# Delta-rule heads with q, k and v projected in a row, k turned later, and adaLN quarters closed in two jobs

## The chip, the cores and the metric

The kernel runs on one core of one Trainium2 chip. A core has TensorE (matmuls and transposes, PE in the profile; its weight loads are PEld), VectorE (DVE), ScalarE (ACT), GpSimd (POOL) and SyncE (SP, which issues most DMAs). Each works through its own queue of instructions in order, and they wait for each other on semaphores. The metric is the device time of one execution in microseconds; of several runs the median counts.

## The reference, cut to what matters

The program is a trunk of two layers over 512 latent tokens behind 256 context tokens, 768 columns in all, with a model width of 2048. Each layer modulates and normalises its input (adaLN), multiplies it by one wide projection matrix, feeds the result to three groups of heads (retention, gated DeltaNet, latent attention), gates each group, and multiplies by an output projection. The change touches the four DeltaNet heads of each layer and the adaLN products. A DeltaNet head is, in the reference:

```python
qkv = jax.nn.silu(centred_dwconv(jnp.concatenate([q, k, v], axis=-1), conv_w))
...
q = l2norm(q) * GDN_HD ** -0.5
k = l2norm(k)
...
kb = k * beta[..., None]
a = jnp.where(strict, jnp.einsum('bhncd,bhnsd->bhncs', kb, k) * decay, 0.0)
rhs = jnp.concatenate([v * beta[..., None], kb * jnp.exp(gc)[..., None]], axis=-1)
sol = lax.linalg.triangular_solve(a + jnp.eye(CHUNK, dtype=f32), rhs, left_side=True,
                                  lower=True, unit_diagonal=True)
```

The convolution has five taps along the tokens. After these lines a scan over the chunks follows, in both directions, with q, k and `sol`. adaLN is a product of the conditioning vectors `c` and `c_ctx` with a 2048 x 6144 matrix in each layer, which gives scale, shift and gate.

## The kernel before, in words

**Numbers and tiles.** Data is float32. For TensorE each operand is split in a high and a low half, and a product is three matmuls: high by high, high by low, low by high. Weights come by DMA as `raw` tiles of 128x512; ACT writes the high half (`wh`, L227) and DVE the low one (`wl`, L228). The normalised input stands in on-chip memory as such halves (`hh`, `hl`). A projection of 128 output rows (`proj_in`, L284 and L286) goes through 16 steps, one for each block of 128 input rows. Each step has six matmuls if the context is needed: three of 512 columns for the latent tokens into `zl`, three of 256 for the context into `zc`. That is 96 matmuls for one projection, or *one tile* in what follows.

**A DeltaNet head** is `gdn_head`. `conv_in` projects, copies the result out of PSUM (`cz`, the context half by DVE, the latent half by ACT at L372), convolves it (the middle tap on ACT at L744, the four others as eight DVE instructions at L751) and applies silu (`ce`, with an exponential on ACT at L396, and a last product on DVE at L400). `gdn_head` calls it for q, then k, then v:

- After q, ACT squares `qT` into `lsq` (L763), and six small matmuls by a column of ones give the sums `ss` (L767).
- After k, six transposes bring `kr` into `knp` with tokens as rows (`turn`, L661). ACT sums the squares, a reciprocal root follows on ACT and DVE (`nss`, `nry`, `nrt`, L375 to L380), and DVE scales to `kn` (L664). Six transposes turn it back into `ktp`, and ACT copies that to `kT` (L778).
- After v, six transposes give `vnp`, copied to `vn`. DVE then writes the exponents `et` and `es` of the decays (12 instructions of each at L803 and L805), and ACT takes their exponentials.
- Then `kkp` (kT by kT on TensorE), `A` (DVE, L820), `Xt` (L833), and the inverse in levels, whose first matmuls are `vtp` (L845). A scan over six chunks in both directions and a normalisation end the head.

**The order of the work.** The kernel is written as Python calls; a scheduler gives each instruction a place in its engine's queue. Work called earlier has precedence, and an instruction whose inputs come later lets later work by. Weight loads run at raised precedence. The mixer phase calls `kr_ab`, four DeltaNet heads and four retention heads, and behind each some of a list `fill` of projections that need no head (query and key compressions, gates, retention's operands): 7, 6, 4 and 5 behind the DeltaNet heads. `gate` of the DeltaNet branch's first output block is called inside head 0 after v. TensorE so finds tiles of other projections to work on while a head's small steps run on DVE and ACT. Head 0 of layer 0 finds its q, k and v projections done in an earlier phase. In layer 1 the heads need q for the latent tokens only.

**adaLN beside the projections.** The 2048 x 6144 products for later use run as 64 jobs, one by each call of `ada_job`, which stands in the middle of every projection (between steps 8 and 9). A job loads parts of the matrix (`araw`), multiplies them on ACT (`ada_p`, L474) and adds them on POOL (`ada_a`, L476). Every fourth job completes a quarter of scale, shift or gate, and the next call of `ada_job` closes it in `ada_close`: matmuls by ones into `ada_z` (L497), a copy to `ada_e` on ACT (L501), four matmuls `ada_q` that turn it (L504), and a DVE add (L505). The jobs end inside layer 0, in its output projection.

Of the kernel before, what the change touches and what calls it, by code (L numbers as in the profile page):

```python
# [20 lines left out]
P = 128  # L21
# [11 lines left out]
C_GDN = 2048  # L33
# [68 lines left out]
def trunk(  # L102
# [19 lines left out]
    def pz(name="z"):  # L122
        return ps.tile([P, 512], F32, name=name, tag="z", bufs=3)

    def pm(name="m"):
        return ps.tile([P, 1024], F32, name=name, tag="m", bufs=2)
# [365 lines left out]
    def ada_close(l, n0):  # L492
        z = pz("ada_z")[:, :256]
        for i, acc in enumerate(ada_accs):
            for v in range(2):
                g = 2 * i + v
                T.matmul(z[32 * g:32 * g + 32], lhsT=ones[:, :32], rhs=acc[:, v], start=True, stop=True,  # L497
                         tile_position=(0, 32 * g))
        ada_accs.clear()
        e = wp.tile([P, 256], F32, name="ada_e", tag="ada_e", bufs=2)  # L500
        S.copy(e, z)  # L501
        q = pz("ada_q")
        for j in range(2):
            T.matmul(q[:, 4 * j:4 * j + 4], lhsT=e[:, j * P:(j + 1) * P], rhs=sel4, start=True, stop=True)  # L504
        V.tensor_tensor(out=ada_t[l][:, n0:n0 + 4, :].rearrange("p (i j) v -> p i j v", j=2),  # L505
                        in0=q[:, :8].rearrange("p (j i v) -> p i j v", j=2, i=2),
                        in1=par[l, 0][:, n0:n0 + 4].rearrange("p (i j) -> p i j", j=2).unsqueeze(3).to_broadcast([P, 2, 2, 2]), op=ALU.add)
        ada_scale(l, n0, 4)

    def ada_job():  # L510
        if 1 in ada_state:
            ada_close(*ada_state.pop(1))
        job = next(ada_jobs, None)
        if job:
            ada_run(job)
# [91 lines left out]
    def phase_a(l, hs):  # L607
        last = l == DEPTH - 1
        parB = par[l, 1]
        if True:  # L610
# [7 lines left out]
            def gate(c0, j):  # L618
                lo_ctx = not last
                zl, zc = proj_in(l, (c0), hs, lo_ctx)  # L620
                z, e = ev("gz"), ev("ge")
                lo = 0 if lo_ctx else NX
                evac(z, zl, zc)
                silu_mul(z[:, lo:], z[:, lo:], e[:, lo:])
                dma(out=gate_d[l][j][:, lo:], in_=z[:, lo:])
# [37 lines left out]
            def scale_tokens(dst, src, r, c0):  # L663
                V.tensor_tensor(out=c6(dst)[:, c0:], in0=c6(src)[:, c0:],  # L664
                                in1=r[:, c0:].unsqueeze(2).to_broadcast([P, NCH - c0, P]), op=ALU.mult)
# [71 lines left out]
            def conv_in(dst, c0, grp, need_ctx):  # L737
                zl, zc = proj_in(l, c0, hs, need_ctx)
                z = ev("cz")
                lo = 0 if need_ctx else NX  # L740
                evac(z, zl, zc)
                y = mk("cy")
                w = lambda j: parB[:, 12 * j + grp:12 * j + grp + 1]
                S.activation(out=y[:, lo:NT], in_=z[:, lo:NT], func=AF.Copy, scale=w(2))  # L744
                for j in (0, 1, 3, 4):
                    o = j - 2
                    for a, b in ((0, NX), (NX, NT)):
                        if a < lo:
                            continue
                        a_, b_ = max(a, a - o), min(b, b - o)  # L750
                        V.scalar_tensor_tensor(out=y[:, a_:b_], in0=z[:, a_ + o:b_ + o], scalar=w(j),  # L751
                                               in1=y[:, a_:b_], op0=ALU.mult, op1=ALU.add)
                e = mk("ce")
                silu_mul(dst[:, lo:NT], y[:, lo:NT], e[:, lo:NT])

            def gdn_head(h, gs):
                be, gcol, egl, ekd, nbe = gs
                qT = pt("qT")
                qlo = NX if last else 0
# [1 line left out]
                qv = tiny("qv")  # L761
                sq = mk("lsq")
                S.activation(out=sq[:, qlo:NT], in_=qT[:, qlo:], func=AF.Square)  # L763
                m = pm("ss")
                c0 = qlo // P
                for n in range(c0, NCH):
                    T.matmul(m[:, n:n + 1], lhsT=sq[:, n * P:(n + 1) * P], rhs=ones[:, 0:1], start=True, stop=True)  # L767
                V.tensor_scalar(out=qv[:, c0:], in0=m[:, c0:NCH], scalar1=EPS, scalar2=EPS * HD, op0=ALU.add, op1=ALU.mult)
                kr = mk("kr")
                conv_in(kr, C_GDN + 512 + h * P, 4 + h, True)  # L770
                kT, kn = pt("kT"), pt("kn")
                m = pm("knp")
                turn(m, kr, 0)
                r = token_rstd(m, 0, kr, lambda ss: V.tensor_scalar(out=ss, in0=ss, scalar1=EPS, scalar2=None, op0=ALU.add))
                scale_tokens(kn, m, r, 0)
                m = pm("ktp")
                turn(m, kn, 0)
                S.copy(kT, m[:, :NT])  # L778
                vT = mk("vT")
                conv_in(vT, C_GDN + 1024 + h * P, 8 + h, True)  # L780
                if h == 0:
                    gate(C_GDN + 1536, 4)

                vn = pt("vn")
                m = pm("vnp")
                for n in range(NCH):
# [269 lines left out]
            fill = cq + gg[1:2] + ckv + gg[2:3] + rr[0] + gg[3:] + rr[1] + rr[2] + rr[3] + mg  # L1056
            nf = [7, 6, 4, 5, 3, 3, 4, 4]
            for i, n in enumerate(nf):
                (gdn_head if i < 4 else ret_head)(*((i, gs) if i < 4 else (i - 4,)))
                for f in fill[sum(nf[:i]):sum(nf[:i + 1])]:  # L1060
                    f()

    def phase_b(l):
# [313 lines left out]
```

## Time and profile before

| | |
|---|---|
| median of 3 runs | 3215.6 us (3211.18 to 3217.71) |
| the profiled execution | 3222.98 us, of it 3221.2 us span |
| granted TensorE clock, mean over the span | 0.976 |
| TensorE busy | 3053.8 us, 95% |
| TensorE's weight loads | 2589.3 us, 80% |
| DVE busy | 2031.1 us, 63% |
| ACT busy | 1657.0 us, 51% |
| POOL busy | 697.1 us, 22% |

Busy shares are of the span. The granted clock is a share of full speed; TensorE runs at one of two levels, 2.4 GHz or 1.2 GHz, and a value between them is a mean over a stretch. In an answer, `PE x <- ACT y` means that TensorE's instruction writing x sat idle until ACT had written y. The times of a timeline count from the start of the span. The 3222.98 us of the profiled execution lie 7.4 us over the median.

### The profile page before, as it was taken

Reading aid. Unit: us, or ns where it says so; the run is one execution under the profiler, and the core shown is the slowest. Engines: PE = TensorE matmul, PEld = TensorE weight load, DVE = VectorE, ACT = ScalarE, POOL = GpSimd, SP = SyncE. Lnnn points to the kernel's source line nnn. Section 1 sums busy time; section 2 is a strip of 40 time slices with the busy share of each in tenths; the row PEclk is TensorE's granted clock in tenths of the full one; section 3 lists DMA queues with packets and bytes.
Section 4 is the critical chain, followed back from the end, with each engine's and each line's share of the span. In section 5 each row is a group of like instructions: output and inputs, shape, how many; then the busy total and the mean of one; then the engine's idle time right before and its main releaser. Section 6 shows DMA issues by size and latency. Waiting matters only on the chain.

```text
span 3221.2 us, 50805 instructions
## 1 busy us (share of the span) xinstructions
PE 3053.8 (95%) x18925; PEld 2589.3 (80%) x18925; DVE 2031.1 (63%) x3524; ACT 1657.0 (51%) x3492; POOL 697.1 (22%) x487
## 2 busy tenths in 40 slices
PE   6998989989889999999999999999999999999998
PEld 3576878878778878899888888888898888888887
DVE  3269568477577566766763355867585767766644
ACT  3266555654555656544677645442424245544534
POOL 0036344443443544000268700000000000000000
PEclk8999999989999999999999999999999999999999
DMA  8763433423424545512465542322323256512444
GB/s 286 257 193 115 122 103 99 133 66 92 134 79 141 159 144 159 159 48 60 136 216 164 160 122 66 98 72 61 102 58 99 74 149 186 147 54 62 134 118 129
DMA packets 496655, 399.22 MB, mean 124 GB/s; under 512 B 45367, under 2 KB 433047, under 8 KB 496407
## 3 DMA queue, kind: packets, MB, share of 16 engines
q1 hardware_dynamic: 496083, 395.87, 41.5%
q8 instruction: 148, 2.42, 0.3%
q14 instruction: 101, 0.82, 0.1%
q0 software_dynamic: 96, 0.02, 0.0%
q10 hardware_dynamic: 227, 0.08, 0.0%
HBM read 340.90 MB, written 54.97 MB: 123 GB/s over the span
## 4 chain that ended last, share of the span: by engine, by line
PE 53%; POOL 2%; ACT 2%; DMA 2%; DVE 2%; issue 1%; SPq 0%; ACTq 0%; POOLq 0%; DVEq 0%
PE zl L284 21%; PE zlc L284 7%; PE zc L286 5%; PE vz L267 4%; PE sc L1157 3%; POOL ada_a L476 2%; PE oacc L1216 2%; PE zt L275 2%; PE zlc L286 1%; PE ptp L1209 1%; PE racc L1037 1%; DMA araw<-in_ada_w_dram 1%; PE f L284 1%; ACT ada_p L474 1%; DMA gb<-g_d 0%
## 5 line engine op out<-in xcount | busy, mean ns | idle before, releaser
L476 POOL TENSOR_TENSOR ada_a<-ada_a,ada_p 128x512 f32<-128x512 f32 x480 | 695.1, 1448 | 1144.8 <-ACT ada_p L474 1098.7
L228 DVE TENSOR_TENSOR wl<-raw,wh 128x512 fp32r<-128x512 f32 x632 | 486.3, 771 | 421.2 <-ACT wh L227 333.1
L227 ACT CAST wh<-raw 128x512 fp32r<-128x512 f32 x632 | 377.8, 605 | 562.0 <-PE zc L286 208.3
L284 PE MATMUL zl<-hh,wh 128*128 128x512 f32 (+1 forms) x1440 | 581.4, 404 | 1.9 <-ACT hh L227 1.8
L284 PE MATMUL zl<-hl,wh 128*128 128x512 f32 (+1 forms) x1440 | 581.3, 404 | 1.0 <-DVE hl L228 1.0
L284 PE MATMUL zl<-hh,wl 128*128 128x512 f32 (+1 forms) x1440 | 581.3, 404 | 0.0
L474 ACT ACTIVATE ada_p<-araw,const_f 128x256 f32<-128x256 f32 x960 | 423.4, 501 | 64.7 <-DMA araw<-in_ada_w_dram 41.3
L284 PEld LDWEIGHTS zl<-hh,wh 128*128 128x128 f32 (+1 forms) x1440 | 274.0, 190 | 64.9 <-issue 3.8
L284 PEld LDWEIGHTS zl<-hh,wl 128*128 128x128 f32 (+1 forms) x1440 | 274.1, 190 | 58.6 <-issue 1.1
L284 PEld LDWEIGHTS zl<-hl,wh 128*128 128x128 f32 (+1 forms) x1440 | 273.8, 190 | 58.6 <-DVE hl L228 2.5
L286 PE MATMUL zc<-hh,wh 128*128 128x256 f32 (+1 forms) x960 | 279.6, 291 | 6.1 <-ACT ce L372 4.9
L286 PE MATMUL zc<-hl,wh 128*128 128x256 f32 (+1 forms) x960 | 277.9, 289 | 0.0
L286 PE MATMUL zc<-hh,wl 128*128 128x256 f32 (+1 forms) x960 | 277.8, 289 | 0.0
L286 PEld LDWEIGHTS zc<-hh,wh 128*128 128x128 f32 (+1 forms) x960 | 183.8, 191 | 14.6 <-ACT ce L372 6.7
L286 PEld LDWEIGHTS zc<-hh,wl 128*128 128x128 f32 (+1 forms) x960 | 184.3, 192 | 3.4 <-issue 2.9
L286 PEld LDWEIGHTS zc<-hl,wh 128*128 128x128 f32 (+1 forms) x960 | 184.5, 192 | 2.6 <-issue 0.8
L284 PE MATMUL zlc<-mh,wl 128*128 128x512 f32 x448 | 178.6, 399 | 0.0
L284 PE MATMUL zlc<-mh,wh 128*128 128x512 f32 x448 | 178.0, 397 | 0.0
L284 PE MATMUL zlc<-ml,wh 128*128 128x512 f32 x448 | 177.3, 396 | 0.0
L751 DVE SCALAR_TENSOR_TENSOR cy<-cz,const_f,cy 128x511 f32<-128x511 f32 (+3 forms) x176 | 141.8, 859 | 17.8 <-ACT cy L744 17.3
L284 PEld LDWEIGHTS zlc<-mh,wh 128*128 128x128 f32 x448 | 84.9, 189 | 20.4 <-ACT ada_p L474 0.8
L284 PEld LDWEIGHTS zlc<-ml,wh 128*128 128x128 f32 x448 | 84.8, 189 | 19.0
(1250 smaller groups left out, 6419.3 us busy)
## 6 DMA issues: line engine op xcount, KB each, us to landing
raw<-in_w_in_dram SPq DMA_DIRECT2D x368, 256.0 KB, 3.6
araw<-in_ada_w_dram SPq DMA_DIRECT2D x256, 256.0 KB, 3.4
raw<-in_w_out_dram SPq DMA_DIRECT2D x144, 256.0 KB, 3.8
ar<-in_ada_w_dram SPq DMA_DIRECT2D x128, 256.0 KB, 5.1
x_d<-xt SPq DMA_DIRECT2D x32, 384.0 KB, 3.6
raw<-in_w_in_dram SPq DMA_DIRECT2D x72, 128.0 KB, 3.4
ret_d<-rw SPq DMA_DIRECT2D x20, 384.0 KB, 2.8
rz<-ret_d SPq DMA_DIRECT2D x20, 384.0 KB, 3.5
```

Of the source, the lines that this page charges most:

```text
L227: S.copy(hi, src)
L228: V.tensor_tensor(out=lo, in0=src, in1=hi.bitcast(F32), op=ALU.subtract)
L267: T.matmul(z[:, 256 * i:256 * i + 256], lhsT=x_[:, (j + i) * P:(j + i + 1) * P], rhs=w, start=first and k == 0 and i == 0, stop=end and k ...
L275: T.matmul(z, lhsT=w, rhs=xx[:, a:b], start=own and first and k == 0, stop=own and last and k == nk - 1)
L284: T.matmul(zl[:m], lhsT=w, rhs=xx[:, NX:], start=st, stop=sp)
L286: i = T.matmul(zc[:m, :NX], lhsT=w, rhs=xx[:, :NX], start=st and zc_open, stop=sp and zc_open)
L474: S.activation(out=pr[:, v], in_=raw[:, i, :], func=AF.Copy, scale=cs32[:, 2 * k + v:2 * k + v + 1])
L476: G.tensor_tensor(out=acc, in0=acc, in1=pr, op=ALU.add)
L751: V.scalar_tensor_tensor(out=y[:, a_:b_], in0=z[:, a_ + o:b_ + o], scalar=w(j), in1=y[:, a_:b_], op0=ALU.mult, op1=ALU.add)
L1037: T.matmul(acc[:, :NL], lhsT=a[:, sl], rhs=b[:, :NL], start=st and i == 0, stop=sp and i == NCH - 1)
L1157: T.matmul(m[:, po:po + n], lhsT=a[:, qs], rhs=b[:, ko:ko + n], start=i == 0, stop=i == len(ops) - 1)
L1216: T.matmul(acc[:, os], lhsT=a[:, sl], rhs=b[:, js], start=j == 0 and n == 0, stop=j == nk - 1 and n == 2)
```

## The change

The program computes the same. Three things move:

- In `gdn_head` the column sums `ss` are called after k's projection and convolution instead of before, and v's after that; only then comes the turning of k into `knp` and `kn`. What is left of k (`ktp`, `kT`) and v's turn follow after one tile of other projections.
- That tile is the new argument `between`: for head 0 the `gate` that stood in it already, for the others the first entry of the head's own share of `fill`.
- `ada_close` ends after the copy to `ada_e`. The `ada_q` matmuls and the add are a function of their own, `ada_turn`, which the following call of `ada_job` runs.

```diff
@@ -499,6 +499,9 @@
         ada_accs.clear()
         e = wp.tile([P, 256], F32, name="ada_e", tag="ada_e", bufs=2)
         S.copy(e, z)
+        return l, n0, e
+
+    def ada_turn(l, n0, e):
         q = pz("ada_q")
         for j in range(2):
             T.matmul(q[:, 4 * j:4 * j + 4], lhsT=e[:, j * P:(j + 1) * P], rhs=sel4, start=True, stop=True)
@@ -508,8 +511,10 @@
         ada_scale(l, n0, 4)
 
     def ada_job():
+        if 2 in ada_state:
+            ada_turn(*ada_state.pop(2))
         if 1 in ada_state:
-            ada_close(*ada_state.pop(1))
+            ada_state[2] = ada_close(*ada_state.pop(1))
         job = next(ada_jobs, None)
         if job:
             ada_run(job)
@@ -753,7 +758,7 @@
                 e = mk("ce")
                 silu_mul(dst[:, lo:NT], y[:, lo:NT], e[:, lo:NT])
 
-            def gdn_head(h, gs):
+            def gdn_head(h, gs, between):
                 be, gcol, egl, ekd, nbe = gs
                 qT = pt("qT")
                 qlo = NX if last else 0
@@ -761,26 +766,24 @@
                 qv = tiny("qv")
                 sq = mk("lsq")
                 S.activation(out=sq[:, qlo:NT], in_=qT[:, qlo:], func=AF.Square)
+                kr = mk("kr")
+                conv_in(kr, C_GDN + 512 + h * P, 4 + h, True)
                 m = pm("ss")
                 c0 = qlo // P
                 for n in range(c0, NCH):
                     T.matmul(m[:, n:n + 1], lhsT=sq[:, n * P:(n + 1) * P], rhs=ones[:, 0:1], start=True, stop=True)
                 V.tensor_scalar(out=qv[:, c0:], in0=m[:, c0:NCH], scalar1=EPS, scalar2=EPS * HD, op0=ALU.add, op1=ALU.mult)
-                kr = mk("kr")
-                conv_in(kr, C_GDN + 512 + h * P, 4 + h, True)
+                vT = mk("vT")
+                conv_in(vT, C_GDN + 1024 + h * P, 8 + h, True)
                 kT, kn = pt("kT"), pt("kn")
                 m = pm("knp")
                 turn(m, kr, 0)
                 r = token_rstd(m, 0, kr, lambda ss: V.tensor_scalar(out=ss, in0=ss, scalar1=EPS, scalar2=None, op0=ALU.add))
                 scale_tokens(kn, m, r, 0)
+                between()
                 m = pm("ktp")
                 turn(m, kn, 0)
                 S.copy(kT, m[:, :NT])
-                vT = mk("vT")
-                conv_in(vT, C_GDN + 1024 + h * P, 8 + h, True)
-                if h == 0:
-                    gate(C_GDN + 1536, 4)
-
                 vn = pt("vn")
                 m = pm("vnp")
                 for n in range(NCH):
@@ -1056,8 +1059,12 @@
             fill = cq + gg[1:2] + ckv + gg[2:3] + rr[0] + gg[3:] + rr[1] + rr[2] + rr[3] + mg
             nf = [7, 6, 4, 5, 3, 3, 4, 4]
             for i, n in enumerate(nf):
-                (gdn_head if i < 4 else ret_head)(*((i, gs) if i < 4 else (i - 4,)))
-                for f in fill[sum(nf[:i]):sum(nf[:i + 1])]:
+                mine = fill[sum(nf[:i]):sum(nf[:i + 1])]
+                if i < 4:
+                    gdn_head(i, gs, gg[0] if i == 0 else mine.pop(0))
+                else:
+                    ret_head(i - 4)
+                for f in mine:
                     f()
 
     def phase_b(l):
```

Line numbers shift: L767 becomes L774, L774 L781, L778 L786, L664 L669, L751 L756, L803 L806. The order of the projections on TensorE is the same tile by tile; the small steps stand elsewhere between their matmuls. Counted in matmuls of a 96-matmul tile, `ss` moves in heads 1 to 3 of layer 0 from the 81st of k's tile to its end, `knp` from the 74th of v's tile to its end, `ktp` from the 5th of the fill tile to its end, `vnp` from the 81st to 85th of the fill tile to its end, `kkp` from there to the 3rd of the tile behind. `vtp` moves in that next tile from the 61st to the 48th in head 1 and from the 77th to the 58th in head 2. `ada_q` stood 5 matmuls behind `ada_z`; now at least half a tile lies between them. SP's and POOL's queues keep their order but for a few rows.

Three places show it, all in head 2 of layer 0. The first is TensorE's queue around `ss`, at the end of k's projection. Before:

```order
L286 MATMUL zc<-hh_1342,wh 128x256
L284 MATMUL zl<-hl_1343,wh 128x512
L767 MATMUL ss<-const_f,lsq 128x1 x6
L286 MATMUL zc<-hl_1343,wh 128x256
L284 MATMUL zl<-hh_1342,wl 128x512
L286 MATMUL zc<-hh_1342,wl 128x256
```

Now; the last two rows belong to v's projection:

```order
L284 MATMUL zl<-hl_1359,wh 128x512
L286 MATMUL zc<-hl_1359,wh 128x256
L284 MATMUL zl<-hh_1358,wl 128x512
L286 MATMUL zc<-hh_1358,wl 128x256
L774 MATMUL ss<-const_f,lsq 128x1 x6
L284 MATMUL zl<-hh_617,wh 128x512
L284 MATMUL zl<-hl_618,wh 128x512
```

`ss` stood inside the 14th of the 16 steps of k's tile and now stands behind the 16th.

The second is DVE's queue around `kn`. `kr` is k after silu, `vT` v after silu, `cy` the convolution's sum, `cz` a projection out of PSUM. Before:

```order
L400 TENSOR_TENSOR kr<-cy,ce 128x768
L228 TENSOR_TENSOR wl<-raw,wh 128x512
L774 TENSOR_SCALAR nss<-nss 128x6
L378 TENSOR_TENSOR nrt<-nrt,nss 128x6
L379 TENSOR_SCALAR nrt<-nrt 128x6
L380 TENSOR_TENSOR nss<-nry,nrt 128x6
L664 TENSOR_TENSOR kn<-knp,nss 128x768
L228 TENSOR_TENSOR wl<-raw,wh 128x512
L371 TENSOR_SCALAR cz<-zc 128x256
L751 SCALAR_TENSOR_TENSOR cy<-cz,const_f,cy 128x254
```

Now:

```order
L756 SCALAR_TENSOR_TENSOR cy<-cz,const_f,cy 128x510
L781 TENSOR_SCALAR nss<-nss 128x6
L228 TENSOR_TENSOR wl<-raw,wh 128x512
L395 SCALAR_TENSOR_TENSOR ce<-cy,ce 128x768
L378 TENSOR_TENSOR nrt<-nrt,nss 128x6
L379 TENSOR_SCALAR nrt<-nrt 128x6
L380 TENSOR_TENSOR nss<-nry,nrt 128x6
L669 TENSOR_TENSOR kn<-knp,nss 128x768
L400 TENSOR_TENSOR vT<-cy,ce 128x768
L806 SCALAR_TENSOR_TENSOR et<-gb,const_f 128x128
```

k's normalisation stood ahead of v's taps and now stands between v's last tap and `vT`.

The third is ACT's queue around `kT`'s copy. `rw<-zl` is the evacuation of the fill tile. Before:

```order
L227 CAST wh<-raw 128x512
L372 ACTIVATE cz<-zl 128x512
L474 ACTIVATE ada_p<-araw,const_f 128x256 x3
L778 COPY kT<-ktp 128x768
L744 ACTIVATE cy<-cz,const_f 128x768
```

Now:

```order
L396 ACTIVATE ce<-ce 128x768
L227 CAST wh<-raw 128x512
L474 ACTIVATE ada_a<-araw,const_f 128x256 x2
L474 ACTIVATE ada_p<-araw,const_f 128x256 x2
L811 ACTIVATE et<-et 128x768
L227 CAST wh<-raw 128x512
L372 ACTIVATE rw<-zl 128x512
L786 COPY kT<-ktp 128x768
L791 COPY vn<-vnp 128x768
L810 ACTIVATE es<-es 128x768
```

The copy stood ahead of v's first tap and now stands behind the fill tile's evacuation, directly ahead of v's own copy.

## Rows read from the trace of the kernel before

**Rows 1.** The page, first part: busy us, share of the span, instructions.

```profile
PE 3053.8 (95%) x18925; PEld 2589.3 (80%) x18925; DVE 2031.1 (63%) x3524; ACT 1657.0 (51%) x3492; POOL 697.1 (22%) x487
```

**Rows 2.** Stretches: us, busy of PE, PEld, DVE, ACT, POOL; clock, DMA, GB/s.

```profile
200.00:1250.00 1050.00, 952.93 (x6238) 823.82 (x6237) 716.85 (x1082) 612.90 (x1377) 467.94 (x322) 0.95 0.41 119
1600.00:1880.00 280.00, 268.35 (x1534) 230.28 (x1535) 123.14 (x155) 177.34 (x386) 190.10 (x133) 0.98 0.54 170
1950.00:2770.00 820.00, 811.72 (x5200) 689.06 (x5200) 561.64 (x1093) 351.11 (x706) 0.00 (x0) 1.00 0.37 102
```

**Rows 3.** Waits of TensorE from 200 to 1250 us: total, times, longest.

```profile
PE ss L767 <- ACT lsq L763: 21.5, 4, 5.7
PE knp L661 <- DVE kr L400: 17.5, 3, 6.0
...
PE ada_q L504 <- ACT ada_e L501: 7.0, 3, 2.9
```

**Rows 4.** Waits of TensorE from 1600 to 1880 us, layer 0's output projection.

```profile
PE ada_q L504 <- ACT ada_e L501: 8.0, 4, 3.9
```

**Rows 5.** Stretches, q's last to v's last matmul, heads 1 to 3.

```profile
412.80:464.80 52.00, 40.64 (x211) 35.30 (x210) 33.45 (x37) 30.24 (x70) 23.00 (x16) 0.87 0.28 80
636.80:689.60 52.80, 41.66 (x211) 36.08 (x210) 33.80 (x38) 30.30 (x71) 23.24 (x16) 0.84 0.23 66
842.00:894.70 52.70, 41.19 (x211) 35.76 (x210) 34.73 (x37) 30.28 (x72) 24.71 (x18) 0.84 0.30 86
```

**Rows 6.** Stretches, v's last matmul to `vtp`; the fourth in layer 1.

```profile
464.80:503.30 38.50, 34.19 (x195) 29.47 (x194) 34.12 (x62) 25.70 (x48) 20.41 (x14) 0.96 0.25 69
689.60:727.00 37.40, 33.45 (x223) 29.76 (x221) 30.93 (x60) 25.30 (x48) 21.70 (x12) 0.95 0.24 64
894.70:935.80 41.10, 34.98 (x206) 29.59 (x204) 33.96 (x63) 26.07 (x49) 16.96 (x13) 0.96 0.23 64
...
2322.20:2349.60 27.40, 27.26 (x184) 24.67 (x182) 23.52 (x60) 15.13 (x22) 0.00 (x0) 1.00 0.04 11
```

**Rows 7.** TensorE's timeline: start, duration, instruction, [idle before <- releaser].

```profile
395.94 0.40 PE L284 MATMUL zl<-hh,wh 128*128 128x512 f32 x1
...
397.00 0.40 PE L284 MATMUL zl<-hh,wh 128*128 128x512 f32 x1
...
656.70 2.50 PE L767 MATMUL ss<-const_f,lsq 128*128 128x1 f32 x11 [5.46 <-ACT lsq L763]
...
682.89 1.51 PE L661 MATMUL knp<-const_f,kr 128*128 128x128 f32 x6 [5.68 <-DVE kr L400]
```

**Rows 8.** ACT's timeline, head 2 of layer 0.

```profile
637.33 0.59 ACT L372 ACTIVATE cz<-zl 128x512 f32<-128x512 f32 x1
...
655.80 0.84 ACT L763 ACTIVATE lsq<-qT 128x768 f32<-128x768 f32 x1
...
691.79 0.78 ACT L778 COPY kT<-ktp 128x768 f32<-128x768 f32 x1
```

**Rows 9.** DVE's timeline, head 2 of layer 0.

```profile
687.37 0.58 DVE L378 TENSOR_TENSOR nrt<-nrt,nss 128x6 f32<-128x6 f32 x1 [1.06 <-ACT nrt L377]
...
689.36 0.96 DVE L664 TENSOR_TENSOR kn<-knp,nss 128x768 f32<-128x768 f32 x1
...
706.69 0.96 DVE L400 TENSOR_TENSOR vT<-cy,ce 128x768 f32<-128x768 f32 x1 [0.98 <-ACT ce L396]
...
718.45 0.34 DVE L820 SCALAR_TENSOR_TENSOR A<-kkp,const_f,es 128x128 f32<-128x128 f32 x1
```

**Rows 10.** What ended idle time before `ada_q`, 690 to 720 us: us, times.

```profile
  ACT ada_e L501: 2.3, 1
```

**Rows 11.** DVE groups (busy, mean ns, idle): 640-950, then 2280-2500 us.

```profile
L751 DVE SCALAR_TENSOR_TENSOR cy<-cz,const_f,cy 128x511 f32<-128x511 f32 x12 | 19.2, 1603 | 0.0
...
L751 DVE SCALAR_TENSOR_TENSOR cy<-cz,const_f,cy 128x511 f32<-128x511 f32 x12 | 9.0, 748 | 0.1
```

## The prediction

> **What bounds the kernel.** I read the busy times first. TensorE is busy for 95% of the span, DVE, the next engine, for 63% (weight loads aside) [rows 1], and the change adds and removes no matmul. What can be won is time in which TensorE waits or runs at its lower clock. So the second view is the stretches: 1050 us of layer 0's mixer phase hold 97 us without a matmul and a granted clock of 0.95; the stretch with the output projection of layer 0 holds 12 us at 0.98; 820 us of layer 1's mixer phase hold 8 us at 1.00 [rows 2]. Third, the waits of layer 0: first come `ss`, the column sums of q's squares (21.5 us, 4 times), then `knp`, k's first transposes (17.5 us, 3 times), then, after smaller ones, `ada_q` (7.0 us, 3 times) [rows 3]. The change is aimed at all three. In the output projection `ada_q` is by far the largest wait: 8.0 us in 4 waits [rows 4].
>
> Head 0 of layer 0 finds its projections done ahead and is a case by itself; heads 1 to 3 are alike. From the last matmul of q to the last matmul of v they need 52.0, 52.8 and 52.7 us with 40.6 to 41.7 us of matmul and a clock of 0.84 to 0.87 [rows 5]. From there to the first inverse matmul (`vtp`) they need 38.5, 37.4 and 41.1 us, at 0.95 to 0.96 [rows 6]. In layer 1, without the adaLN work, head 2 needs 27.4 us for the latter, and TensorE is idle for 0.1 us of it [rows 6].
>
> **q, k, v in a row.** A projection with context has 16 steps of 1.06 us (397.00 − 395.94) [rows 7], 17.0 us. In head 2, q's last matmul is at 636.8; its evacuation on ACT starts at 637.33 and `lsq` ends at 655.80 + 0.84 = 656.64 [rows 8]: a chain of 19.8 us. Before, `ss` stood behind 81 of k's 96 matmuls, and TensorE waited 5.46 us [rows 7]; now it stands behind all 96, so some 17.0 us lie in front of it and 2.8 us of wait remain. `ss` itself took 2.5 us at the half clock [rows 7], 1.3 at the full one. Then v runs, 17.0 us, with `knp` now behind all 96 of its matmuls instead of 74. k's chain is about as long as q's, and it begins late on DVE, whose queue still holds qT and two products with it when k ends; but `ss` has given it 4 us more. I take no wait at `knp`. A wait of 2.8 us still costs some clock: stretches with 4 to 6 us of idle time show 0.95 to 0.96, so 1.5 to 1.9 us are lost [rows 6]; I take 1.7. New stretch: 17.0 + 2.8 + 1.3 + 17.0 + 1.7 = 39.8 us, against 52.5 on average. **Gain 3 × 12.7 = 38 us.** If k's late start shows at `knp` (3.5 us a head), 27; if neither wait is left, 51.
>
> **Turning k and v.** Now v's chain carries k's tail. On DVE the steps from `nrt` to `kn` take 690.32 − 687.37 = 2.95 us [rows 9], and they stand between v's `ce` and vT, partly beside an exponential of v on ACT for which DVE waited 0.98 us before [rows 9]: vT comes 1.9 us later. After vT nothing is saved by the order: 24 `et`/`es` rows, the fill tile's evacuation, then `A`. Before, `A` came 718.45 − 707.65 = 10.8 us after vT, two weight splits included [rows 9]; now one split and one 0.4 us evacuation lie there, 8 to 9 us. On ACT kT's copy (0.78 us [rows 8]) stands behind the exponential of `et`, which must wait for about half of these 24 rows; I put it 6.4 us after vT. `kkp` then waits some 5 us on TensorE, but DVE reaches `A` only 2 us later, so most of this wait is time that would have been lost at `vtp`. The stretch to `vtp` so stays as long as it was, about 39 us: later vT and earlier `A` cancel. What is lost is work: `vtp` now stands 58 instead of 77 matmuls into the next tile in head 2, 48 instead of 61 in head 1, and head 3 is like them, about 2.2 us at the pace of [rows 7]. **Loss 3 × 2.2 = 6.6 us** (nothing if `A` comes 2 us earlier; 20 if v's chain grows by 4.5 us a head).
>
> The fill tile is no extra work: the projections follow each other on TensorE as before, only the small steps stand elsewhere. Its DMAs and adaLN jobs keep their places to a few rows on SP, and the POOL adds keep their order. Head 0 of layer 0, where `ss` moves by 1 us: nothing (±2).
>
> **adaLN in two jobs.** `ada_q` now stands at least half a projection (8.5 us) behind `ada_z`, where 5 matmuls lay between; the longest wait was 3.9 us, so none is left. Of 8.0 + 7.0 us [rows 4, 3] the 2.3 us in head 2 [rows 10] and the 2.9 in head 3 [rows 3] lie in a stretch whose end the chain on DVE sets, and save nothing. 9.8 us remain, and the clock: 0.02 × 280 = 5.6 us at most in the output projection [rows 2], and some 1.7 in layer 0's heads. Of 16 to 17 us **I take 14**, because ACT, which makes the copy, also waits there for POOL (190.10 us busy in the stretch [rows 2]) and makes the weight splits, so that a part may come back as a late split. Ends: 3 and 16.5.
>
> **Layer 1** had no wait to lose. Head 2's 27.4 us without idle time [rows 6] now hold k's tail, `kn` and the fill's evacuation on DVE ahead of `A`, 2 to 3 us, while TensorE has about 1.6 us more work ahead of `vtp`. I take 1.5 us for each of heads 1 to 3 and 1.5 for the rest: **loss 6 us** (0 to 15, with clock drops).
>
> **Sum.** 38 − 6.6 + 14 − 6 = 39 us. The profiled execution took 3222.98 us (span 3221.2 and 1.8 around it), so 3184; it lies 7.4 us over the median of the runs, 3215.6, and I take the gain off that: **3177 us**.
>
> **A rule against this change.** In layer 0 a 511-column tap of the convolution takes 1603 ns, in layer 1 748 [rows 11]; POOL, which makes the adaLN adds, is busy there for 17 to 25 us of each stretch of heads 1 to 3 and not at all in layer 1 [rows 5, 6]. The Trainium skill, "SBUF — State Buffer", section "Who interferes with whom", says that a DVE instruction with two SBUF inputs and a GpSimd instruction that reads SBUF block each other for a whole instruction. By that rule the trace agrees, and v's convolution would pay too wherever the adds now fall on it. The mechanism has a price from the rows: 2 × 0.86 us for the widest taps, up to 4 us with the others, so 12 us over three heads, on the chain that sets `vtp`. That is rival 1.
>
> **Rivals.** (1) The adds fall on v's taps, and vT comes up to 4 us later in heads 1 to 3: 3177 + 12 = 3189. For it: TensorE faster, the same adds in less time. Against: their order on ACT and POOL is unchanged. (2) `ada_q`'s wait comes back at the weight splits of the output projection, since ACT waits for POOL there either way: 3177 + 14 = 3191. Against: ACT waited for TensorE to free split buffers in most of that stretch, so it is ahead. (3) Slower: the tail is not covered. One place, the stretch from v's last matmul to `vtp`: k's normalisation stands whole in front of vT (7.4 us in head 2, from `knp` at 682.89 to the end of `kn` at 690.32 [rows 7, 9]) and kT's copy comes late (5.7 us), both on top; a little over half of it in layer 1. 3 × 13.1 + 4 × 7.6 = 70 us against 38 + 14 − 6.6 = 45: 3241. It decides where that stretch grows by over 6.5 us in each of seven heads. Against: DVE needs its 24 rows before `A` anyway, and kT's copy fits beside them. (4) Gain and loss cancel, because the steps shift the wait from `ss` and `knp` to `kkp` one for one: 3216. (5) No wait is left at `ss`: 3163.
>
> **How the numbers follow.** Forecast 0.62, rivals 1 to 5: 0.10, 0.12, 0.07, 0.05, 0.04. The four terms go down by 11, 13, 11 and 9 us and up by 13, 7, 2.5 and 6; taken as independent, 22 and 16 us, so 3161 to 3199 for the forecast alone. The range of 8 in 10 takes in rivals 1 and 2 with their own spread: 3160 to 3207. A measurement of this kernel can tell about 0.2%, 6.4 us, from no change. Faster by more than that: 0.62 + 0.10 + 0.12 + 0.04 = 0.88; within: 0.05; slower: 0.07.
>
> **What would show it.** Right: heads 1 to 3 need about 40 us from q's last to v's last matmul at a clock of 0.95 or more; `ss` waits near 3 us, `knp` under 2; `ada_q` waits nowhere; a new wait of about 5 us at `kkp` in heads 2 and 3; the stretch to `vtp` stays within 36 to 42 us. Wrong: waits of 5 us left at `ss`, a wait for `vT` or `kn` of more than 4 us, `vtp` more than 6 us later after v's end than before, layer 1's mixer phase longer by over 15 us, or new waits for splits in the output projection.

## The result, and the profile after

The changed kernel takes 3193.29 us (median of 4 runs, 3190.64 to 3194.6), the kernel before 3216.25 (4 runs). The ratio is 0.9926, with a 95% interval of 0.9912 to 0.994: 23 us faster. The forecast was 39 us less, 3177, in a range of 3160 to 3207. The profiled execution took 3192.3 us, 3190.5 of them span. Between the two first profiles lie 30.7 us, more than between the medians, since that execution of before was a long one.

The page of the changed kernel, busy times; TensorE's share is that of [rows 1], with 14 us less of it:

```profile
PE 3040.1 (95%) x18925; PEld 2581.0 (81%) x18925; DVE 2027.6 (64%) x3524; ACT 1650.6 (52%) x3492; POOL 697.6 (22%) x487
```

Stretches after, columns as in [rows 2]: first from q's copy out of PSUM to v's in heads 1 to 3 (`cz` on ACT; each window begins and ends 0.5 us ahead of it), then from there to `vtp`. In the kernel before, a copy starts within 0.3 us of its projection's last matmul, so that [rows 5] and [rows 6] show the same stretches:

```profile
414.80:458.30 43.50, 40.02 (x218) 34.77 (x216) 33.88 (x34) 27.35 (x53) 21.94 (x15) 0.92 0.34 95
634.30:676.70 42.40, 38.73 (x215) 33.20 (x214) 31.68 (x34) 26.77 (x53) 20.30 (x14) 0.96 0.30 85
831.60:873.50 41.90, 39.38 (x214) 34.30 (x212) 31.63 (x33) 26.70 (x53) 20.91 (x15) 0.92 0.32 93
458.30:498.30 40.00, 32.38 (x182) 27.65 (x182) 35.43 (x65) 27.75 (x65) 20.21 (x15) 0.96 0.29 82
676.70:715.00 38.30, 32.12 (x201) 28.60 (x199) 32.50 (x63) 27.30 (x66) 19.95 (x15) 0.91 0.31 86
873.50:912.10 38.60, 32.10 (x187) 27.48 (x186) 33.20 (x65) 27.77 (x67) 19.97 (x15) 0.96 0.32 93
```

Between the copies, the row of three projections fell from about 52.5 to 42 or 43 us, and the stretch behind it kept its length, but for head 3. Between last matmuls, which is how the prediction counts, the row fell further, from 52.1, 52.8 and 52.8 to 40.9, 39.4 and 40.7 us, and the stretch from v's last matmul to `vtp` grew from 38.2, 37.1 and 40.8 to 42.1, 40.7 and 39.2. The two counts differ because v's copy now starts 1.1 to 2.9 us behind v's last matmul. In head 2 that matmul and k's transposes on TensorE are

```profile
674.02 0.28 PE L286 MATMUL zc<-hh,wl 128*128 128x256 f32 x1
675.46 0.85 PE L666 MATMUL knp<-const_f,kr 128*128 128x128 f32 x6 [1.16 <-DVE kr L400]
```

and ACT, which makes v's copy (the last row), still has k's exponential, two weight casts and five adaLN products ahead of it in its queue:

```profile
673.41 0.85 ACT L396 ACTIVATE ce<-ce 128x768 f32<-128x768 f32 x1 [1.02 <-DVE ce L395]
674.16 0.60 ACT L227 CAST wh<-raw 128x512 fp32r<-128x512 f32 x1
674.67 2.10 ACT L474 ACTIVATE ada_p<-araw,const_f 128x256 f32<-128x256 f32 x5
676.68 0.60 ACT L227 CAST wh<-raw 128x512 fp32r<-128x512 f32 x1
677.19 0.59 ACT L372 ACTIVATE cz<-zl 128x512 f32<-128x512 f32 x1
```

Waits of TensorE after, 200 to 1250 us, as [rows 3]:

```profile
PE vtp L855 <- DVE vt L849: 12.5, 8, 2.9
PE ss L774 <- ACT lsq L768: 11.2, 4, 4.1
PE ot L666 <- DVE osq L669: 9.3, 5, 3.7
...
PE kkp L820 <- ACT kT L786: 6.1, 2, 5.8
...
PE knp L666 <- DVE kr L400: 2.2, 3, 1.2
```

`ss` fell from 21.5 to 11.2 us, `knp` from 17.5 to 2.2, and `ada_q` is gone from this stretch. In their place `vtp`, `ot` (the turn in a head's last normalisation) and `kkp` wait longer. In the output projection the 8.0 us at `ada_q` [rows 4] became waits of its own matmuls (`zlc`) for splits and for the adaLN copy. The changed kernel, 1580 to 1880 us:

```profile
PE zlc L284 <- ACT ada_e L501: 2.5, 1, 2.5
PE zlc L284 <- DVE wl L228: 2.1, 2, 1.0
PE ptp L1216 <- DVE mx L1169: 1.7, 1, 1.7
PE ada_q L507 <- ACT ada_e L501: 1.1, 1, 1.1
PE zlc L284 <- ACT wh L227: 1.1, 2, 0.9
```

### The profile page after: what moved, and what is told of

Same layout as the page of the kernel before. It is cut to its first block, busy times and chain, and to the rows that moved or that the text cites. A ratio compares the mean times of both kernels' runs of the same rounds, so it can differ in the third digit from the quotient of the medians.

```text
span 3190.5 us, 50748 instructions
## 1 busy us (share of the span) xinstructions
PE 3040.1 (95%) x18925; PEld 2581.0 (81%) x18925; DVE 2027.6 (64%) x3524; ACT 1650.6 (52%) x3492; POOL 697.6 (22%) x487
## 5 line engine op out<-in xcount | busy, mean ns | idle before, releaser
L228 DVE TENSOR_TENSOR wl<-raw,wh 128x512 fp32r<-128x512 f32 x632 | 478.0, 760 | 406.3 <-ACT wh L227 303.7
L756 DVE SCALAR_TENSOR_TENSOR cy<-cz,const_f,cy 128x511 f32<-128x511 f32 (+3 forms) x176 | 145.2, 879 | 14.3 <-ACT cy L749 14.0
L284 PEld LDWEIGHTS zlc<-mh,wl 128*128 128x128 f32 x448 | 84.1, 188 | 20.9 <-DVE wl L228 3.1
(1250 smaller groups left out, 6410.5 us busy)
```

Of the source, the lines that this page charges most:

```text
L228: V.tensor_tensor(out=lo, in0=src, in1=hi.bitcast(F32), op=ALU.subtract)
L284: T.matmul(zl[:m], lhsT=w, rhs=xx[:, NX:], start=st, stop=sp)
```

## Experiments: the three parts alone and in pairs

The change has three parts: the *sums* (`ss` behind k's projection), the *turns* (k turned behind v's projection, with the fill tile), and the *quarters* (adaLN closed in two jobs). Each time below stands beside runs of before on the same chip, and each ratio with its 95% interval; the changed kernel was not run beside the kernels below, so it is compared by its 23 us.

**The quarters alone.** The kernel before with

```diff
         S.copy(e, z)
+        return l, n0, e
+
+    def ada_turn(l, n0, e):
         q = pz("ada_q")
...
```

> Before, with only the closing of the adaLN quarters in two jobs (the heads as before). Forecast's term: 14 us less than before, 3202. Theory from the two traces: the waits at ada_q go, but about half comes back as late weight splits in the output projection (9 us are gained there by the changed kernel, from -24.4 to -33.5), and in layer 0's heads next to nothing: 9 to 11 us less, 3206. Rival: the splits take all of it back, 0 to 3 us less. In the trace: no wait at ada_q over 1.2 us, and in the output projection waits for wh, wl or ada_e of 5 to 7 us in all.

Measured: 3204.53 us against 3212.8, ratio 0.9976 (0.9967 to 0.9984): 8 us, a little under the theory's 9 to 11 and well under the forecast's 14. The output projection's waits came back as splits, 6.8 us in these three lines of 1590 to 1870 us:

```profile
PE zlc L284 <- ACT ada_e L501: 3.2, 1, 3.2
PE zlc L284 <- DVE wl L228: 2.3, 3, 1.0
...
PE zlc L284 <- ACT wh L227: 1.3, 3, 0.9
```

**The heads without the quarters** (the changed kernel with the diff above taken back).

> The changed kernel with each adaLN quarter closed in one job again; the heads stay changed. Forecast: heads and layer 1 give 25 us, so 3191. Theory from the traces: the measured 23 us less the 9 to 11 of adaLN leave 12 to 14 us, so 3203. Rival (the two parts help each other, because ada_q stands in the rows of q, k and v): under 8 us. In the trace: from q's last to v's last matmul 42 to 44 us in heads 1 to 3 of layer 0, and ada_q's waits in the output projection back at 8 us with a clock of 0.98.

Measured: 3208.17 us against 3212.8, 0.9987 (0.9978 to 0.9995): only 4.6 us. The rival's size holds: heads and quarters give 8 + 5 apart and 23 together. Its reason does not: the row of projections is as short as in the changed kernel (table below). `ada_q` waits 10.6 us in layer 0, 3.6 more than in [rows 3], but its two long waits (4.6 and 4.5 us) stand between v and `vtp`, a stretch that is 116.3 us long here and 115.6 in the changed kernel. What differs lies behind `vtp`, where `ot` waits 11.8 us:

```profile
PE ss L769 <- ACT lsq L763: 13.4, 4, 5.4
PE ot L661 <- DVE osq L664: 11.8, 6, 3.6
PE ada_q L504 <- ACT ada_e L501: 10.6, 3, 4.6
```

**The sums alone.** The kernel before with

```diff
+                kr = mk("kr")
+                conv_in(kr, C_GDN + 512 + h * P, 4 + h, True)
                 m = pm("ss")
...
-                kr = mk("kr")
-                conv_in(kr, C_GDN + 512 + h * P, 4 + h, True)
```

> Before, with only the column sums of q moved behind k's projection; k is still turned before v is projected. Theory: the waits at ss and at knp are two separate halves of the gain. Here ss waits 2 to 3 us instead of 5.5 and knp still about 6, so the stretch from q's last to v's last matmul is 48 to 49 us in heads 1 to 3 against 52.5, some 10 to 12 us less in all. Rival: the wait at knp grows by what ss gives back, since k's chain on DVE then begins behind q's rest: within 3 us of before. Rival 2: ss carries nearly all of it: 20 us or more.

Measured: 3197.48 us, 0.9958 (0.9945 to 0.997): 15 us, more than the theory's 10 to 12. The row needs 48.1, 47.1 and 47.6 us, so its 14.7 us account for the gain. Two moved lines give three times what all the heads' edits give together, and these two intervals do not overlap.

**Sums and quarters, without the turns.**

> Before, with the column sums of q behind k's projection and the adaLN quarters in two jobs; k is turned before v, as before. The heads alone gave 4 us and the quarters alone 8, the whole change 22 to 23: 10 us more than their sum. Theory: the two small waits (sums, quarters) are what pays, 15 and 8 us, and add up; turning k behind v's projection adds little. Then 23 us less than before here, 3190, the same as the changed kernel. Rival: the quarters pay more only where k is turned behind v, since only there ada_q stands in the heads' row of projections: then 15 us less or fewer, 3198 or more. Rival 2: as with the heads, some of the sum is lost between the inverse and the next head's q, 18 us less.

Measured: 3186.28 us against 3214.24, 0.991 (0.9895 to 0.9924): 28 us, more than the whole change. The theory that the turns add nothing fell on the side of a loss, if a small one: 0.991 and the changed kernel's 0.9926 have intervals that overlap.

**Turns and quarters, without the sums.** The changed kernel with the `ss` lines ahead of k's projection.

> The changed kernel with the column sums of q ahead of k's projection again: k turned behind v, and adaLN in two jobs. Theory: turning k behind v's projection gives about nothing net, since the 6 us at knp come back as a stretch between vtp and the next head's q; with adaLN's 8 us this is 3203 to 3206. Rival: the turns carry half of the heads' gain, 3198. In the trace: from q's last to v's last matmul about 47.5 us in heads 1 to 3 of layer 0 (ss waits 5, knp under 1.5).

Measured: 3210.07 us, 0.9985 (0.9976 to 0.9994): 4 us less than before, where the quarters alone give 8. That is above the theory's band and its rival's time. So the turns cost 4 us here, 5 beside sums and quarters (23 for 28) and 11 beside the sums alone (4.6 for 15). Only the 11 are clear of the intervals; the other two pairs point the same way.

**Layer 1's heads as before**, in the changed kernel (`if last:` the old order, `else:` the new one).

> The changed kernel with the heads of layer 1 in the order of before (sums, k turned, v, no fill tile between). Forecast: layer 1 loses 6 us by the change, so 3187. Theory from the traces: its mixer phase lost about 3 us, most of it at a wait of 4.7 us for the sums in head 1 of layer 1: 3190. Rival: what that wait costs is given back within the phase, 3193, the same as the changed kernel. In the trace: no wait at ss over 2 us in layer 1.

Measured: 3190.91 us, 0.9928 (0.9914 to 0.9942), and 0.9926 for the changed kernel: they can't be told apart. In the traces layer 1 from head 0's q to a projection behind head 3 (its first matmul is at 2534.3 us in before) takes 564.5 us before, 567.5 changed and 563.6 here; `ss` waits 1.3 us in all instead of 6.6.

**Before, profiled again.**

> The kernel of before, profiled again. Its first profiled execution took 3222.98 us, above every one of 23 runs on another chip (up to 3219.2). Theory: some 8 us of the 30.7 us between the spans of the two first profiles belong to that execution: here a span of 3207 to 3216, with about 5 us less at the start (before head 0's q) and the rest in clock in layer 0. Rival: a profiled execution is always this long, 3221.

Measured: 3202.68 us, a span of 3200.9, below the theory's band and below every timed run beside it (3210.02 to 3223.48). Profiled executions of one kernel so lie 20 us apart. What differs is the start (2.8 us), the stretch from head 3's inverse to the end of the phase (8.7 us) and some clock. The row of projections repeats to 0.4 us in each head (52.4, 52.8, 52.7). What follows on single stretches rests on differences that repeat in several kernels; the stretch behind head 3's inverse does not repeat, and a few us there mean nothing.

## Where the turns lose

The table splits layer 0 by two events of each head: the first copy of a projection out of PSUM on ACT (`cz`, L372) and the first `vtp`. Lengths in us are worked out from the timelines; "row" and "v to vtp" are sums over heads 1 to 3. "The phase's end" stands for the fourth projection of latent attention's compressed input (`ch`), whose first matmul is at 1444.9 us in before, and "output projection" for the stretch from the seventh of these to the 24th of the output projection's 28 tiles (1581.2 to 1837.3 us in before). A star marks a stretch with the event described under it.

| stretch | before | again | sums | quarters | sums, quarters | sums, turns | turns, quarters | all |
|---|---|---|---|---|---|---|---|---|
| row, q to v | 157.5 | 157.8 | 142.8 | 156.2 | 141.3 | 126.6 | 142.1 | 127.7 |
| v to `vtp` | 115.5 | 113.3 | 114.0 | 114.5 | 113.6 | 116.3 | 116.1 | 115.6 |
| `vtp` of head 0 to q of 1 | 136.2 | 134.8 | 135.0 | 142.8* | 145.2* | 133.6 | 140.5* | 141.1* |
| `vtp` of 1 to q of 2 | 134.0* | 134.0* | 133.3* | 125.9 | 127.2 | 139.0* | 136.2* | 136.5* |
| `vtp` of 2 to q of 3 | 115.5 | 113.4 | 113.6 | 112.2 | 112.8 | 125.7* | 117.3 | 117.1 |
| `vtp` of 3 to the phase's end | 509.1 | 500.5 | 506.7 | 508.2 | 503.9 | 515.8 | 506.7 | 508.4 |
| output projection | 256.1 | 255.7 | 256.9 | 252.1 | 252.0 | 252.7 | 251.7 | 247.3 |

The turns shorten the row by 13.6 us beside sums and quarters (141.3 to 127.7). They save 4.1 behind head 0's inverse and 4.7 in the output projection. They lose 2.0 between v and `vtp`, 9.3 behind head 1's inverse, 4.2 behind head 2's, 4.5 behind head 3's (where traces of one kernel differ by 8.7) and, in layer 1, 6.7 (560.8 to 567.5), of which 4.1 in the row of its second head, where `ss` came to wait 4.7 us. For the largest loss the trace shows a wait and what ends it. ACT's queue in the changed kernel, near the end of head 1 (`nry`, `nrt`: the reciprocal root of its last normalisation; `qe`: the exponential of the *next* head's decays, which waits for the DMA of `gb`):

```profile
580.45 0.21 ACT L375 ACTIVATE nry<-nss 128x6 f32<-128x6 f32 x1 [0.23 <-DVE nss L946]
580.69 0.21 ACT L376 ACTIVATE nry<-nry 128x6 f32<-128x6 f32 x1
584.27 0.84 ACT L813 ACTIVATE qe<-gb 128x768 f32<-128x768 f32 x1 [3.38 <-DMA gb<-g_d]
585.02 0.19 ACT L377 ACTIVATE nrt<-nry 128x6 f32<-128x6 f32 x1
```

What TensorE pays for it 2 us later, in the turn that the normalisation feeds:

```profile
586.87 0.87 PE L666 MATMUL ot<-const_f,osq 128*128 128x128 f32 x6 [3.67 <-DVE osq L669]
```

ACT at the same place with sums and quarters but without the turns; `ot` there waits for nothing the profile shows:

```profile
582.37 0.20 ACT L375 ACTIVATE nry<-nss 128x6 f32<-128x6 f32 x1
582.60 0.21 ACT L376 ACTIVATE nry<-nry 128x6 f32<-128x6 f32 x1
582.84 0.21 ACT L377 ACTIVATE nrt<-nry 128x6 f32<-128x6 f32 x1
...
587.32 0.85 ACT L815 ACTIVATE qe<-gb 128x768 f32<-128x768 f32 x1 [4.26 <-DMA gb<-g_d]
```

The next head's exponential stands between two steps of this head's chain and holds the second until its transfer lands. The kernel before has the same in head 1:

```profile
586.47 0.84 ACT L810 ACTIVATE qe<-gb 128x768 f32<-128x768 f32 x1 [4.54 <-DMA gb<-g_d]
587.22 0.19 ACT L377 ACTIVATE nrt<-nry 128x6 f32<-128x6 f32 x1
```

Where the scheduler puts it changes from kernel to kernel. In all fourteen traces of this study a star goes with a wait of 3.3 to 4.6 us at that `ot`, and heads 0 and 1 have none without it. With the clock that follows, a starred stretch is 6 to 8 us longer than the same stretch without the star (before and the kernel with sums against the two kernels with quarters and no turns, head 1: 133.3 to 134.0 against 125.9 to 127.2). Before has one star, the quarters move it from head 1 to head 0, and the turns add a second. So 9.3 us behind head 1 are, by estimate, about 7 of this and 2.3 of work moved (13 matmuls of 0.177 us). The wait is shown; that a star costs 6 to 8 us is argued from kernels that differ in other edits too, since no run moves `qe` alone.

**Is it contention with the POOL adds?** An alternative for the turns' loss was that the inverse's DVE steps now lie beside adaLN's adds. Three kernels have the adds on 16 columns, which leaves out most of the adaLN product:

```diff
-                    G.tensor_tensor(out=acc, in0=acc, in1=pr, op=ALU.add)
+                    G.tensor_tensor(out=acc[:, :, :8], in0=acc[:, :, :8], in1=pr[:, :, :8], op=ALU.add)
```

> Before, with each POOL add of adaLN on 16 columns instead of 512: most of the adaLN product is left out, and the queues keep nearly their order. It is the base for the next two. Theory (DVE's instructions stretch beside POOL's adds): 511-column taps of the convolution take 750 ns in layer 0 too instead of 1603, and the run is 30 to 50 us shorter, 3165 to 3185. Rival (POOL costs only through its own lateness): taps stay at 1600 ns and the run is within 10 us of before.

> The kernel with the sums behind k and adaLN in two jobs, k turned before v, with the same POOL adds on 16 columns. Theory: without the adds less is waited for at ss, so the two together win 10 to 20 us over before with small adds, where they won 28 with the adds. Rival: 28 again.

> The changed kernel with the POOL adds on 16 columns; TensorE's queue is the same as in the changed kernel. It lost 5 us to the kernel without the turns when both had the whole adds. Theory: the turns lose because the inverse's DVE instructions come to lie beside POOL adds (in head 1 ten of one kind took 11.7 us instead of 7.1); without the adds the turns win what the wait at knp cost, and this kernel is 4 to 10 us faster than the one without the turns and the same small adds. Rival: they lose by the order alone (the inverse starts 13 to 16 matmuls earlier in its tile, kT stands behind exponentials on ACT): 5 us slower again, or more.

Measured: 3073.82 us for before with small adds (0.9569 of before, 0.9556 to 0.9582), 3063.11 for sums and quarters (0.9534), 3069.87 for the whole change (0.9559). The taps take 746 ns, as the first theory said, but the run is 138 us shorter where it said 30 to 50. Sums and quarters win 10.7 us over before with small adds, as the second theory said. The turns lose again, by 6.8 us and clear of the runs' spread, with the adds all but gone: the rival, loss by the order alone, holds, and the third theory fell. Both stars are there, and `ot` waits as before:

```profile
539.08 1.33 PE L666 MATMUL ot<-const_f,osq 128*128 128x128 f32 x5 [3.70 <-DVE osq L669]
```

The change as a whole is worth 4 us here, within the intervals, instead of 23. The reason is in the waits of before with small adds, 190 to 1160 us: one wait at `ss` is left, head 0's, and next to none at `knp`.

```profile
PE ss L767 <- ACT lsq L763: 5.9, 1, 5.9
PE ot L661 <- DVE osq L664: 4.3, 2, 4.0
...
PE knp L661 <- DVE kr L400: 0.7, 2, 0.4
```

From the start of q's copy to the end of `lsq` before needs 19.3 us (637.33 to 656.64 in the prediction's rows) and 13.9 without the whole adds (head 1: 386.61 to 400.54). The waits that the change hides exist because the adds stretch the chain on DVE.

## Two candidates

**The sums behind v's projection**, in the changed kernel:

> The changed kernel with the column sums of q behind v's projection instead of k's. Nothing needs them before the end of the head. Theory: TensorE's 2.2 to 2.5 us at ss and the clock behind it (1.7 to 3.4 us) go in heads 1 to 3 of layer 0, and 3 to 6 us at head 0 and layer 1's second head: from q's last to v's last matmul 39 to 40 us, in all 10 to 16 us less than the changed kernel, 3180. Rival: the chain on DVE sets the end of the head anyway, so the wait shows up at the inverse and only 0 to 4 us are won, 3190.

Measured: 3182.63 us against 3214.24, 0.991 (0.9892 to 0.9927): 32 us less than before, where the changed kernel is 23 less; the two intervals overlap. What the theory took for won in layer 0 is not. v's last matmul does come 34.2, 33.9 and 33.6 us behind q's, but v's copy comes 8.4 to 9.2 us behind it, so between the copies the row stays (43.4, 42.4, 42.2 us): `ss` no longer waits in heads 1 to 3, and `knp` waits instead. Waits from 200 to 1250 us:

```profile
PE knp L666 <- DVE kr L400: 18.1, 4, 5.9
...
PE ss L776 <- ACT lsq L768: 3.8, 1, 3.8
```

Between the copies the row keeps k's chain as its length, whichever wait shows it. The clearest gain is in layer 1, 9.7 us (557.8 for 567.5), most of it the row of the second head, 40.1 instead of 48.4.

**The sums behind v's projection, k turned early, quarters in two jobs:**

> A candidate: k turned before v as in the kernel of before, q's sums behind v's projection, adaLN in two jobs. Theory: in layer 0 the wait only moves from ss to knp, as it did when the changed kernel's sums went behind v (knp 5.9 us again), so its heads stay as with the sums behind k; layer 1 saves the 3.5 us at ss in its second head and the clock behind it. 3 to 5 us less than with the sums behind k, some 30 us less than before: 3183. Rival: with two waits merged into one the clock falls for longer, and it is the same or worse, 3186 to 3192.

Measured: 3191.25 us against 3212.32, 0.9931 (0.9917 to 0.9944). The theory's part on layer 0 holds (row 140.3 us, as with the sums behind k), but the time is worse, as the rival said. The theory's saving in layer 1 was not there to be had: in the trace with the sums behind k `ss` does not wait in layer 1's second head (1.2 us, in head 0, is all), since that wait came with the turns; layer 1 takes 564.1 us here for 560.8 there. In layer 0 `knp` alone now waits 39.5 us in 4 waits, up to 10.7, where the theory had 5.9. Why the whole is slower stays open. The kernel with sums and quarters alone and the changed kernel with its sums behind v are the best found, both at 0.991 of before.

## The prediction, point by point

- **What bounds it.** Right. The three waits named are those that went, and the row of projections is where the heads gained.
- **q, k, v in a row.** The mechanism is right: `ss` waits 2.2, 2.4 and 2.5 us (forecast 2.8) and `knp` 0.3, 1.2 and 0 (none). From q's last matmul to v's the heads need 40.9, 39.4 and 40.7 us (forecast 39.8), 36.7 us less than before in all (forecast 38). The granted clock of 0.95 was missed in two heads: it is 0.92, 0.96 and 0.92, so 1.6 to 3.3 us are lost where 1.7 was taken.
- **v to `vtp`.** The stretch was to keep its length, since a later vT and an earlier `A` cancel. From v's last matmul it grew by 5.9 us, from 116.1 to 122.0, and in head 1 it is 42.1, just outside the 36 to 42 named. The working delayed vT by 1.9 us for k's normalisation and counted nothing for v's copy, which starts 1.1 to 2.9 us behind v's last matmul. Between the copies the gain of the row is 29.8 us and the stretch behind keeps its length (115.5 and 115.6). `kkp` waits 5.8 us in head 2 alone, where heads 2 and 3 were named; in head 3 a context matmul waits 4.5 us for ACT (`rw`) instead.
- **Work moved behind `vtp`.** The matmuls were counted about right (13 + 19 + 14 of 0.177 us, 8.1 us for 6.6). The step that failed is what the sum left out: it took the stretches from `vtp` to the next head's q as moved work alone. There the turns cost 9.3 and 4.2 us behind heads 1 and 2 and save 4.1 behind head 0; the 4.5 behind head 3 are less than two traces of before differ by. The two stars were not in any rival, though the row of before in which ACT waits 4.5 us for `gb` between `nry` and `nrt` (at 586.47) was there to be found. By the times, the sums alone win 15 us, and the turns, which were to win the other half at `knp`, take 11 of them back.
- **adaLN in two jobs.** 14 us forecast, 8 alone. Rival 2's mechanism took place in part, and with it one of the signs of being wrong: new waits for splits and for the adaLN copy in the output projection, 5.7 us in the changed kernel and 6.8 with the quarters alone. In layer 0 the gain behind head 1 (8 us, its star goes) is lost behind head 0 (7 us, a star comes). Beside the heads the quarters are worth 18 us (23 less than before with them, 4.6 without); the traces, 12.8 us apart, put 5.4 of it in the output projection, 7.4 behind head 3 and 2.5 behind head 1, while the star that goes from head 2 comes back behind head 0. Behind head 3 the kernel without the quarters waits 3.3 and 2.5 us at `ot` and 1.5 at `ada_q`, which the changed kernel does not; whether that is the 7.4 us stays open.
- **Layer 1.** Forecast a loss of 6; 3.0 in the traces, with a place that was not foreseen: `ss` in its second head.
- **A rule against this change.** Rival 1 put up to 4 us a head, 12 in all, on v's taps. They take 8.0 us in each of heads 1 to 3 instead of 7.0 to 7.2, so it took place at a fifth of its size. The price of one tap was right, 857 ns: a 511-column tap takes 746 ns in layer 0 with small adds, 1603 with whole ones [rows 11]. What the prediction did not see is what the adds cost the whole kernel (last section). The Trainium skill, "SBUF — State Buffer", section "Who interferes with whom", says that a DVE instruction with two SBUF inputs contends with a GpSimd instruction that reads SBUF; these runs agree for the 511-column taps, while the 510-column ones, with the same kinds of input, only went from 826 ns to 746 without the whole adds.
- **Sum.** In the traces: 2.0 up to head 1's q, -29.8 in the rows, 0.1 to `vtp`, 4.0 behind heads 1 and 2, -0.7 behind head 3, -8.9 from the output projection to layer 1, 3.0 in layer 1, -0.4 at the end: -30.7, with the rows taken between the copies. With an execution of before that is not long it is less, 23 by the medians. The forecast's direction and range hold; it is 16 us too low mainly because it booked the wait at `knp` as won, which the turns give back elsewhere. That it came this near is in part luck: the heads with layer 1 were to give 25 us and give 4.6 alone, the quarters 14 and give 8, and about 10 of the 23 come only when both are there, from places (stars that go and come, the stretch behind head 3) that no term of the sum holds.

Not tried: holding `qe` back until the normalisation ahead of it is done, or loading `gb` earlier. By the table it would give the changed kernel some 14 us; that is argued, not shown.

## What to carry to other kernels

Split a change into its parts before believing its sum: here two moved lines won 15 us, and a larger reordering beside them lost 4 to 11 (the 4 within the noise). When work is moved so that a wait is covered, follow the chain to its next use as well, and look in the in-order queues of the other engines for an instruction of later work that waits for a DMA in the middle of the current chain. A wait on TensorE that another engine's slow chain causes can also be attacked at what slows the chain.

## What was not expected of the hardware

The adaLN adds on POOL cost far more than any wait named in the profile of before. With 16 columns instead of 512 in each add the program, otherwise the same, takes 138 us less (3073.8 for 3212.3), while POOL's busy time falls by 543 us and DVE's, for the same instructions, by 191. The page of before with small adds:

```profile
PE 3001.7 (98%) x18925; PEld 2553.1 (83%) x18925; DVE 1839.9 (60%) x3524; ACT 1651.0 (54%) x3492; POOL 154.2 (5%) x487
```

The queues issue the same work on ACT and the same DMAs. Most of the difference is in the mixer phase of layer 0, where DVE's taps, splits and spreads run beside the adds, and 20 us are in the output projection (236.6 for 256.1).
